# A hybrid decoder step on one core: half of the weight rests on GpSimd up to the MLP, the first weight blocks in halves, the convolution as a side job

## The chip, the cores and the metric

The kernel runs on one core of a Trainium2 chip. The metric is the device time of one execution in microseconds (us); less is better. Before the change three runs took 1318.51, 1319.54 and 1319.89 us, median 1319.54.

## The reference

One layer of a decoder for 256 prompt tokens and 8 x 8 sample tokens, 320 tokens in all, in float32, at a width of 2048:

```
z = rmsnorm(x, g_mix) @ w_in                      # 2048 x 3584: b, c, h, q, k, v, qx
u = c * h;  y_conv = b * short_conv(u, conv_w)    # three taps; the samples start from a cache
y_swa = sink_attention(rmsnorm(q), rmsnorm(k), v, rel_bias, sinks)   # window 128, 8 heads
mk, mv = rmsnorm(mem) @ w_mem_k (normed), @ w_mem_v                  # 256 memory tokens
y_x = softmax(rmsnorm(qx) mk) mv                  # 4 heads; the samples read a cache
x = x + concat(y_conv, y_swa, y_x) @ w_out        # 2048 x 2048
x = x + relu(rmsnorm(x, g_mlp) @ w_up)^2 @ w_down # 2048 x 8192, 8192 x 2048
```

Returned are x and the new cache rows (convolution, keys, values).

## The kernel before

**The matrix products.** Activations lie transposed, 16 blocks of 128 features by 320 tokens. Each float32 operand is split into a high part that the matmul's fp32r type holds exactly and the rest: `S0h`, `S0l` and `S1h`, `S1l` for activations, `wh`, `wl` for weights. A product is three matmuls, high x high, low x high and high x low, the last of which reads `wl`.

**Weight pieces.** The weights come in 360 pieces of 256 rows x 512 columns (512 KB). `load_piece` starts the transfer of a piece into one of four `raw` tiles on SP's queue. `split_piece` has ScalarE write `wh` (`act.activation ... Copy`) and notes a function `rest`, in which VectorE writes `wl = raw - wh` and which then starts the load of the piece four further on into the `raw` tile that this frees. Four `wh`/`wl` pairs exist, so the split of piece i waits for the last matmul on piece i - 4.

**Units.** A group is 512 output columns, four PSUM tiles `mm` (m = 0 to 3); it takes 8 pieces (`w_out` in two parts of 4). `add_group` cuts it into units of 12 matmuls: at a group's start and end one m with two pieces, between them two m with one piece. The very first group starts with units of two m and one piece. `run_unit` issues a unit, then calls `split_piece` and `boundary`, which lets the due evacuations and rests be issued and steps the side jobs. The groups in order: qx, then k and v, the memory keys and values (matmuls of 512 columns), q (two groups), c, h, b, `w_out`, and four times `w_up` and `w_down`. `split_piece` starts with pieces 0 and 1; the first of them is split in two halves.

**Side jobs.** Everything else on TensorE (norms, attention, transposes, in PSUM tiles `ax`) is a Python generator that `Side.step` moves on by a step between units. A job waits in its program position until `Pace`, a model with a clock for each engine and a cost for each operation, says that its tiles are ready (`after`). The model decides only where an instruction stands in the order; on the chip each engine executes its own instructions in that order and waits on semaphores. `bias_job` builds the relative bias: transfers on GpSimd's queue, then a matmul `ax<-w,z` on the tile `hot` that holds `in_c_hot`. Its `dve.memset` of `bt` stands in VectorE's order after the rest of piece 7, and the transfers on GpSimd's queue wait for it.

**The convolution.** `c_evac` and `h_evac` run when the groups c and h end. `h_evac` for each m forms h, multiplies it into `u` and applies the three taps at once, on VectorE. `b_evac` multiplies by b.

**Where things are recorded.** All operations are issued through `Paced`, so that nearly all rows of the profile have one line, L166. Tiles tell them apart.

Of the kernel before, what the change touches and what calls it, by code (L numbers as in the profile page):

```python
# [9 lines left out]
F32 = mybir.dt.float32  # L10
# [23 lines left out]
NW2 = 12  # L34
LAG = 6.0
WARM = 9
C_B, C_C, C_H, C_Q, C_K, C_V, C_X = 0, 512, 1024, 1536, 2560, 2816, 3072
# [55 lines left out]
class Pace:  # L93
# [12 lines left out]
    def cost(self, eng, op, out, ins):  # L106
        n = max(a.free_size() for a in [out] + ins)
        if eng == "pe":
            n = out.free_size()
            if ins[0].dtype == F32R:  # L110
                return 0.0033 + n / 2400.0
            quarter = 0.25 if out.partition_size() == 32 else 1.0
            return 0.0009 * n if op == "transpose" else max(0.11, n / 600.0) * quarter
        if eng == "act":
            return 0.1 + n * 0.00083
        if eng == "dve":
            return 0.08 + n * 0.00104
        return 0.1 + n * 0.0025
# [15 lines left out]

    def load(self, out):
        start = max(self.clock["dma"], self.clock["pe"])
        self.clock["dma"] = start + out.free_size() * 4 * out.partition_size() / 330e3
        self.wrote[out.name] = (self.clock["dma"] + (2.0 if out.name.startswith("raw") else LAG), "dma")

# [7 lines left out]
class Paced:  # L147
# [3 lines left out]
    def __getattr__(self, op):  # L151
        f = getattr(self.engine, op)
        if not callable(f) or op == "preload_act_table_set":
            return f

        def issue(*args, **kw):
            aps = [a for a in list(kw.values()) + list(args) if isinstance(a, bass.AP)]
            out = kw["out"] if "out" in kw else args[0]
            if op == "dma_start":
                if out.name not in self.pace.dram:  # L160
                    self.pace.load(out)
            else:
                if "accum_out" in kw:
                    self.pace.wrote[kw["accum_out"].name] = (self.pace.clock[self.name] + 0.5, self.name)
                self.pace.issue(self.name, op, out, [a for a in aps if a is not out])
            return f(*args, **kw)  # L166

        return issue
# [79 lines left out]
def trunk_step(ctx: ExitStack, tc: tile.TileContext, I, O):  # L248
# [26 lines left out]

    def bank():
        return ax.need([P, 512])

# [18 lines left out]
    ident = const.tile([P, P], F32, name="ident")  # L297
    act.dma_start(out=ident, in_=I["c_ident"])
    col, off = {}, 0
# [96 lines left out]
    def load_piece():  # L396
        i = count["load"]
        if i >= len(pieces):
            return
        count["load"] += 1  # L400
        w, k0, c0 = pieces[i]
        t = raw_p.tile([P, 2, 512], F32, name="raw", tag="raw")
        for c in [slice(0, 2)] if i else [slice(0, 1), slice(1, 2)]:
            sp.dma_start(out=t[:, c, :], in_=w[c0 // 512, k0 // 2][:, c, :])
        wt[i] = t

    def split_piece():
# [8 lines left out]
        wt[i] = (h, l)  # L416
        if not i:
            for c in range(2):
                side.until([f"x0{c}"])
                act.activation(out=h[:, c, :], in_=r[:, c, :], func=AF.Copy)  # L420
                dve.tensor_tensor(out=l[:, c, :], in0=r[:, c, :], in1=h[:, c, :].bitcast(F32), op=ALU.subtract)
            load_piece()
# [9 lines left out]
    def add_group(w, c0, korder, a, evac, kind="std", needs=None, pre=None, k0=0):  # L432
# [36 lines left out]
    def run_unit(un):  # L469
# [9 lines left out]
        ah, al = un["act"]()  # L479
        if un["kind"] == "std":  # L480
            for m in un["ms"]:
# [38 lines left out]

    def load_x(b, cuts=((0, 4),)):
        t = lx.must([P, 4, T])
        for lo, hi in cuts:
            sp.dma_start(out=t[:, lo:hi, :], in_=I["xT"][:, 4 * b + lo:4 * b + hi, :])
        xblk[b] = t

# [9 lines left out]
    def x_job():  # L536
        for i in range(8):
            for k in (2 * i, 2 * i + 1):
                split_act(S0h[:, k, :], S0l[:, k, :], xblk[k // 4][:, k % 4, :], gcol("g_mix", k))
                if not i:  # L540
                    side.flags.add(f"x0{k}")
                    yield 1
            side.flags.add(f"x{i}")
            yield 1
# [294 lines left out]
    def cross_sample(f):  # L839
# [92 lines left out]
    def swa_prompt(g, hp):  # L932
# [7 lines left out]
        for blk in range(2):  # L940
# [20 lines left out]
            yield 1  # L961
            pt = yield from half()
            act.activation(out=pt[:, 0:2 * nk], in_=bk[:, 0:2 * nk], func=AF.Copy)
            ax.put(bk)
            w2.put(s)
            yield from after(pt, vnat)
# [146 lines left out]
    def conv_pre_job():  # L1113
        st["u"] = yield from lx.need([P, 4, UC])
        cc = yield from half()
        pool.memset(st["u"][:, :, 0:2], 0.0)
        sp.dma_start(out=cc[:, 0:64], in_=I["cconv"].rearrange("p m r -> p (m r)"))
        yield from after(cc)
# [3 lines left out]
        w2.put(cc)  # L1122

    def h_evac(m, ps):
# [28 lines left out]
    def b_evac(m, ps):  # L1153
        side.until(["cp"])
        y = st["y"][m]
# [148 lines left out]
    side.add("cp", cross_prompt_all(), needs=xq + ["mk", "mix"], cost=2, heavy=1)  # L1304
    side.add("convpre", conv_pre_job(), needs=["rb", "mix"], cost=1)
    side.add("cs1", cross_sample(1), needs=xq + ["cs0"], cost=6, heavy=2)
    for g in range(2):
        qn = [f"q{g * 4 + h}" for h in range(4)]
        for i in range(2):
            side.add(f"swp{g}{i}", swa_prompt(g, i), needs=qn + [f"k{g}", f"v{g}", "bias", "cp"], cost=3, heavy=1)  # L1310
    for g in range(2):
        qn = [f"q{g * 4 + h}" for h in range(4)]
        for i in range(2):
            side.add(f"sws{g}{i}", swa_sample(i, g), needs=qn + [f"k{g}", f"v{g}", "biass", "cp"], cost=2, heavy=1)

    split_piece()
    side.until(["x1"])
    split_piece()
    flush(subs)
    for un in units:  # L1320
# [46 lines left out]
```

## Time and profile before

| what | value |
|---|---|
| profiled execution | 1319.31 us, span 1316.8 us |
| runs shown | 1318.51, 1319.54, 1319.89 us |
| TensorE busy | 1309.4 us, 8954 matmul records |
| VectorE busy | 675.2 us |
| ScalarE busy | 540.5 us |
| GpSimd busy | 17.7 us, 36 instructions |
| granted TensorE clock | 1.0 over the span |

2.5 us of the profiled execution lie outside its span. A matmul's record reaches from its start to its modelled end and overlaps the next one, so TensorE's pace is read from the distance of the starts, and a wait of TensorE from a distance that is larger than the pace. "[0.78 <-DMA w<-in_c_hot]" behind a row of the timeline says how long the engine was idle before it and what ended that. In such rows `w`, `z`, `lx`, `ax`, `mm` are families of buffers.

### The profile page before, as it was taken

Reading aid. Unit: us, or ns where it says so; the run is one execution under the profiler, and the core shown is the slowest. Engines: PE = TensorE matmul, PEld = TensorE weight load, DVE = VectorE, ACT = ScalarE, POOL = GpSimd, SP = SyncE. Lnnn points to the kernel's source line nnn. Section 1 sums busy time; section 2 is a strip of 40 time slices with the busy share of each in tenths; the row PEclk is TensorE's granted clock in tenths of the full one; section 3 lists DMA queues with packets and bytes.
Section 4 is the critical chain, followed back from the end, with each engine's and each line's share of the span. In section 5 each row is a group of like instructions: output and inputs, shape, how many; then the busy total and the mean of one; then the engine's idle time right before and its main releaser. Section 6 shows DMA issues by size and latency. Waiting matters only on the chain.

```text
span 1316.8 us, 21550 instructions
## 1 busy us (share of the span) xinstructions
PE 1309.4 (99%) x8954; PEld 1286.9 (98%) x8954; DVE 675.2 (51%) x1022; ACT 540.5 (41%) x801; POOL 17.7 (1%) x36
## 2 busy tenths in 40 slices
PE   9999999999999999999999999999999999999998
PEld 8988999999999999999999999999999999999998
DVE  6876666776576444444344444344443344444342
ACT  7784554343355344332244432234442324433321
POOL 1011000000000000000000000000000000000000
PEclk9999999999999999999999999999999999999999
DMA  8667545366344444444444444444444444444552
GB/s 310 240 200 267 189 165 200 109 220 250 128 145 161 145 152 136 160 147 158 146 155 133 152 159 154 147 157 129 160 154 152 153 151 128 161 154 152 176 167 72
DMA packets 65025, 217.03 MB, mean 165 GB/s; under 512 B 8374, under 2 KB 10142, under 8 KB 64897
## 3 DMA queue, kind: packets, MB, share of 16 engines
q1 hardware_dynamic: 62896, 210.38, 47.8%
q0 software_dynamic: 1744, 5.19, 1.1%
q8 instruction: 70, 1.15, 0.4%
q14 instruction: 27, 0.21, 0.0%
q10 hardware_dynamic: 288, 0.10, 0.0%
HBM read 211.53 MB, written 7.65 MB: 166 GB/s over the span
## 4 chain that ended last, share of the span: by engine, by line
PE 98%; DMA 1%; DVE 0%; SPq 0%; ACT 0%; issue 0%; POOL 0%; DVEq 0%
PE mm L166 95%; PE ax L166 3%; DMA raw<-in_w_in 0%; DMA w<-in_c_hot 0%; DVE wl L166 0%; SPq L166 0%; ACT wh L166 0%; POOL z L166 0%; DVE lx L166 0%; DVE S0l L166 0%; DVEq L166 0%; DVE z L166 0%
## 5 line engine op out<-in xcount | busy, mean ns | idle before, releaser
L166 DVE TENSOR_TENSOR wl<-raw,wh 128x1024 fp32r<-128x1024 f32 (+1 forms) x361 | 435.9, 1220 | 479.8 <-ACT wh L166 473.2
L166 ACT ACTIVATE wh<-raw 128x1024 fp32r<-128x1024 f32 (+1 forms) x361 | 374.1, 1052 | 629.5 <-PE mm L166 591.0
L166 PE MATMUL mm<-S0h,wh 128*128 128x320 f32 x1472 | 458.1, 311 | 0.4 <-ACT wh L166 0.4
L166 PE MATMUL mm<-S0h,wl 128*128 128x320 f32 x1472 | 455.3, 309 | 1.6 <-DVE wl L166 1.6
L166 PE MATMUL mm<-S0l,wh 128*128 128x320 f32 x1472 | 454.8, 309 | 0.0
L166 PE MATMUL mm<-S1h,wh 128*128 128x320 f32 x1280 | 397.3, 310 | 0.0
L166 PE MATMUL mm<-S1h,wl 128*128 128x320 f32 x1280 | 395.5, 309 | 0.0
L166 PE MATMUL mm<-S1l,wh 128*128 128x320 f32 x1280 | 395.5, 309 | 0.0
L166 PEld LDWEIGHTS mm<-S0h,wh 128*128 128x128 f32 x1472 | 276.4, 188 | 3.8 <-issue 2.7
L166 PEld LDWEIGHTS mm<-S0h,wl 128*128 128x128 f32 x1472 | 276.3, 188 | 2.6 <-DVE wl L166 2.6
L166 PEld LDWEIGHTS mm<-S0l,wh 128*128 128x128 f32 x1472 | 276.5, 188 | 0.1
L166 PEld LDWEIGHTS mm<-S1h,wh 128*128 128x128 f32 x1280 | 240.3, 188 | 0.7 <-issue 0.6
L166 PEld LDWEIGHTS mm<-S1l,wh 128*128 128x128 f32 x1280 | 240.3, 188 | 0.1
L166 PEld LDWEIGHTS mm<-S1h,wl 128*128 128x128 f32 x1280 | 240.2, 188 | 0.0
L166 DVE TENSOR_TENSOR lx<-mm,lx 128x320 f32<-128x320 f32 x96 | 46.9, 489 | 78.7 <-PE mm L166 78.6
L166 ACT ACTIVATE z<-z 128x320 f32<-128x320 f32 (+1 forms) x118 | 54.9, 469 | 65.3 <-DVE z L166 64.2
L166 DVE TENSOR_TENSOR S1l<-z,S1h 128x320 fp32r<-128x320 f32 x68 | 33.4, 491 | 51.8 <-ACT S1h L166 51.8
L166 ACT ACTIVATE S1h<-z 128x320 fp32r<-128x320 f32 x68 | 32.1, 471 | 8.1 <-DVE z L166 6.1
L166 DVE SCALAR_TENSOR_TENSOR z<-mm,r2b 128x320 f32<-128x320 f32 x64 | 31.0, 484 | 0.0
L166 PE MATMUL mm<-wh,S1h 128*128 128x512 f32 x64 | 25.6, 400 | 0.0
L166 PE MATMUL mm<-wh,S1l 128*128 128x512 f32 x64 | 25.1, 392 | 0.0
L166 PE MATMUL mm<-wl,S1h 128*128 128x512 f32 x64 | 25.0, 391 | 0.0
(160 smaller groups left out, 431.2 us busy)
## 6 DMA issues: line engine op xcount, KB each, us to landing
raw<-in_w_up SPq DMA_DIRECT2D x128, 512.0 KB, 3.3
raw<-in_w_down SPq DMA_DIRECT2D x128, 512.0 KB, 3.3
raw<-in_w_in SPq DMA_DIRECT2D x55, 512.0 KB, 4.3
raw<-in_w_out SPq DMA_DIRECT2D x32, 512.0 KB, 3.5
raw<-in_w_mem_k SPq DMA_DIRECT2D x8, 512.0 KB, 4.5
raw<-in_w_mem_v SPq DMA_DIRECT2D x8, 512.0 KB, 3.4
w<-in_cmk SPq DMA_DIRECT2D x16, 256.0 KB, 5.3
w<-in_cmv SPq DMA_DIRECT2D x16, 256.0 KB, 5.2
```

Source lines behind the costliest of these rows:

```text
L166: return f(*args, **kw)
```

## The change

1. **Rests on GpSimd.** For the even pieces 8 to 102 (48 of them) `rest` issues `wl = raw - wh` on GpSimd in place of VectorE.
2. **The start.** Pieces 0 and 1 are both split in halves, with the activation blocks 0 to 3 split between the halves; the transfers are issued block by block in the order in which they are used, the first of x on ScalarE's queue. The first four units take one half of a piece for all four m, as four high x high, four low x high and four high x low matmuls. Ten in place of nine warming matmuls on `ones` stand ahead. `ident` is loaded on GpSimd's queue.
3. **Model.** The costs in `Pace` are changed, a transfer that is issued on GpSimd's queue counts as ready after 10 us in place of 6, others after 5; that moves side jobs in the order.
4. **Convolution.** The three taps leave `h_evac` for a side job, `conv_job`. The cache rows of the convolution are loaded with the bias.
5. **Smaller moves.** The x blocks that `w_out` adds to are loaded one group at a time. Two memsets go from GpSimd to VectorE. The last of the 16 output blocks is added and stored in two halves, on two queues.

```diff
-LAG = 6.0
-WARM = 9
+LAG = 5.0
+WARM = 10
+POOLED = 8, 104
...
-        if not i:
+        if i < 2:
+
             for c in range(2):
-                side.until([f"x0{c}"])
+                k = 2 * i + c
+                x = xblk[0][:, k, :]
+                if k:
+                    split_act(S0h[:, k, :], S0l[:, k, :], x, gcol("g_mix", k))
+                else:
+                    dve.tensor_scalar(out=S0h[:, k, :], in0=x, scalar1=gcol("g_mix", k), scalar2=None, op0=ALU.mult)
+                    dve.scalar_tensor_tensor(out=S0l[:, k, :], in0=x, scalar=gcol("g_mix", k),
+                                             in1=S0h[:, k, :].bitcast(F32), op0=ALU.mult, op1=ALU.subtract)
                 act.activation(out=h[:, c, :], in_=r[:, c, :], func=AF.Copy)
                 dve.tensor_tensor(out=l[:, c, :], in0=r[:, c, :], in1=h[:, c, :].bitcast(F32), op=ALU.subtract)
...
+        eng = pool if not i % 2 and POOLED[0] <= i < POOLED[1] else dve
+
         def rest():
-            dve.tensor_tensor(out=l, in0=r, in1=h.bitcast(F32), op=ALU.subtract)
+            eng.tensor_tensor(out=l, in0=r, in1=h.bitcast(F32), op=ALU.subtract)
             load_piece()
...
-                ends[0] = [([2 * q, 2 * q + 1], [i]) for i in range(2) for q in range(2)]
+                ends[0] = [(list(range(4)), [i]) for i in range(2) for _ in range(2)]
...
+            for n, (w, x) in enumerate(((h, ah), (h, al), (l, ah))):
+                for m in un["ms"]:
+                    pe.matmul(out=grp[m][:, 0:T], lhsT=w[:, j, m * P:(m + 1) * P], rhs=x[:, k, :],
+                              start=u == 0 and n == 0, stop=False)
...
         dve.memset(bt[0:33, 0:8], 1.0)
+        pool.dma_start(out=ident, in_=I["c_ident"])
         pool.dma_start(out=bt[0:32, 0:8], in_=I["rel_bias_table"])
         pool.dma_start(out=hot[0:33, 0:384], in_=I["c_hot"])
         pool.dma_start(out=skb, in_=I["sinks"].to_broadcast([P, NH]))
         pool.dma_start(out=sel, in_=I["c_sel"])
+        pool.dma_start(out=cc, in_=I["cconv"].rearrange("p m r -> p (m r)"))
         pool.dma_start(out=gkx, in_=I["g_k_x"].to_broadcast([P, P]))
...
-        dve.tensor_scalar(out=z, in0=u[:, m, 0:336], scalar1=gcol("conv_w", m), scalar2=None, op0=ALU.mult)
-        for i in (1, 2):
-            dve.scalar_tensor_tensor(out=z, in0=u[:, m, i:i + 336], scalar=gcol("conv_w", 4 * i + m), in1=z,
-                                     op0=ALU.mult, op1=ALU.add)
-        st["y"][m] = z
+        zs.put(z)
         if m == 3:
-            side.add("convout", conv_out_job())
+            side.add("convy", conv_job())
...
+            if last and g == 3 and m == 3:
+                for queue, c in ((act, slice(0, T // 2)), (sp, slice(T // 2, T))):
+                    dve.tensor_tensor(out=a[:, c], in0=ps[:, c], in1=a[:, c], op=ALU.add)
+                    queue.dma_start(out=O["yT"][:, KT - 1, c], in_=a[:, c])
+                return
...
-    load_x(0, ((0, 2),))
+    load_x(0, 0, 1, act)
     load_piece()
-    sp.dma_start(out=xblk[0][:, 2:4, :], in_=I["xT"][:, 2:4, :])
     load_piece()
-    load_x(1, ((0, 2), (2, 4)))
+    for k in range(4):
+        if k:
+            load_x(0, k, k + 1, sp)
+        load_part(k // 2, slice(k % 2, k % 2 + 1))
+    load_x(1, 0, 2, sp)
     load_piece()
...
```

How the change moves instructions, at the places on which the prediction rests. On GpSimd, before, from the transfers of the bias job (`z` is `bt`, `w_4` is `hot`) to the store of the biases:

```order
L166 DMA z_346<-in_rel_bias_table 32x8
L166 DMA w_4_347<-in_c_hot 33x384
L166 DMA skb<-in_sinks 128x8
L166 DMA sel<-in_c_sel 128x4
L166 DMA gkx<-in_g_k_x 128x128
L166 MEMSET w_5_435 128x512
L166 MEMSET w_6_436 128x512
L166 DMA rv_d<-w_11_486 8x384
```

And in the changed kernel:

```order
L169 DMA z_352<-in_rel_bias_table 32x8
L169 DMA w_4_353<-in_c_hot 33x384
L169 DMA skb<-in_sinks 128x8
L169 DMA sel<-in_c_sel 128x4
L169 DMA cc<-in_cconv 128x64
L169 DMA gkx<-in_g_k_x 128x128
L169 ISA
L169 TENSOR_TENSOR wl<-raw,wh 128x1024
L169 MEMSET w_5_445 128x512
L169 MEMSET w_6_446 128x512
L169 TENSOR_TENSOR wl<-raw,wh 128x1024
L169 DMA rv_d<-w_12_517 8x384
```

One transfer more, the first two rests (pieces 8 and 10), and ahead of the first of them an instruction of a kind of its own, ISA, which this place of the program before does not have. In the built program that row is a reload of GpSimd's code library, number 0.

On TensorE around the matmul of the bias, before: it stands behind 168 matmuls on weights, 24 ahead of the end of the first group:

```order
L166 MATMUL mm<-S0h,wh 128x320
L166 MATMUL mm<-S0l,wh 128x320
L166 MATMUL mm<-S0h,wl 128x320
L166 MATMUL ax_460<-w_4_347,z_346 8x384
L166 MATMUL mm<-S0h,wh 128x320
```

And in the changed kernel, where it stands behind 180:

```order
L169 MATMUL mm<-S0h,wh 128x320
L169 MATMUL mm<-S0l,wh 128x320
L169 MATMUL mm<-S0h,wl 128x320
L169 MATMUL ax_489<-w_4_353,z_352 8x384
L169 MATMUL mm<-S0h,wh 128x320
```

The twelve matmuls of one unit have moved ahead of it, and the rest of piece 8 is read 14 matmuls behind it in place of 26.

On VectorE in the group h, before, the last convolution of `h_evac` and the rests of pieces 66, 67 and 68:

```order
L166 TENSOR_TENSOR z_2944<-mm,rb 128x320
L166 TENSOR_TENSOR lx_1375<-z_2944,lx_1375 128x256
L166 TENSOR_TENSOR lx_1375<-z_2944,lx_1375 128x8x8
L166 TENSOR_SCALAR z_2944<-lx_1375,cols 128x336
L166 SCALAR_TENSOR_TENSOR z_2944<-lx_1375,cols,z_2944 128x336 x2
L166 TENSOR_TENSOR wl<-raw,wh 128x1024
```

And in the changed kernel:

```order
L169 TENSOR_TENSOR z_3029<-mm,rb 128x320
L169 TENSOR_TENSOR lx_1381<-z_3029,lx_1381 128x256
L169 TENSOR_TENSOR lx_1381<-z_3029,lx_1381 128x8x8
L169 TENSOR_SCALAR z_3036<-lx_1381,cols 128x336
L169 SCALAR_TENSOR_TENSOR z_3036<-lx_1381,cols,z_3036 128x336 x2
L169 TENSOR_TENSOR S1l<-ax_2957,S1h 128x4x32
L169 TENSOR_TENSOR S1l<-ax_2959,S1h 128x4x32
L169 TENSOR_TENSOR wl<-raw,wh 128x1024
```

The `wl` in the first of these is piece 66, in the second piece 67; piece 66 is now GpSimd's. Of the four convolutions one stands ahead of it in place of four.

More of the change, by code (lines that the diff above doesn't have):

```diff
@@ L133, in issue, with load @@
                 self.read[k] = (end, eng)
-    def load(self, out):
+    def load(self, out, queue):
         start = max(self.clock["dma"], self.clock["pe"])
-        self.clock["dma"] = start + out.free_size() * 4 * out.partition_size() / 330e3
-        self.wrote[out.name] = (self.clock["dma"] + (2.0 if out.name.startswith("raw") else LAG), "dma")
+        self.clock["dma"] = start + out.free_size() * 4 * out.partition_size() / 410e3
+        self.wrote[out.name] = (self.clock["dma"] + (2.0 if out.name.startswith("raw") else 2 * LAG if queue == "pool" else LAG), "dma")
     def ready(self, tiles):
@@ L160, in issue @@
                 if out.name not in self.pace.dram:
-                    self.pace.load(out)
+                    self.pace.load(out, self.name)
             else:
                 if "accum_out" in kw:
-                    self.pace.wrote[kw["accum_out"].name] = (self.pace.clock[self.name] + 0.5, self.name)
+                    self.pace.wrote[kw["accum_out"].name] = (self.pace.clock[self.name] + 0.9, self.name)
                 self.pace.issue(self.name, op, out, [a for a in aps if a is not out])
+                if "accum_out" in kw:
+                    self.pace.clock[self.name] += 0.19
             return f(*args, **kw)
@@ L274, in after, with bank @@
             yield 1
-    def bank():
-        return ax.need([P, 512])
+    def bank(every=1):
+        while side.now % every:
+            yield 1
+        t = ax.get([P, 512])
+        while t is None:
+            yield every
+            t = ax.get([P, 512])
+        return t
     def zt(cols=336):
@@ L400, in load_piece, with load_part @@
         count["load"] += 1
+        wt[i] = raw_p.tile([P, 2, 512], F32, name="raw", tag="raw")
+        if i > 1:
+            load_part(i, slice(0, 2))
+    def load_part(i, c):
         w, k0, c0 = pieces[i]
[L402 to L405, printed above, removed]
+        sp.dma_start(out=wt[i][:, c, :], in_=w[c0 // 512, k0 // 2][:, c, :])
     def split_piece():
@@ L519, in trunk_step, with load_x @@
     xblk, mblk = {}, {}
[L521 to L525, printed above, removed]
+    def load_x(b, lo, hi, queue):
+        if b not in xblk:
+            xblk[b] = lx.must([P, 4, T])
+        queue.dma_start(out=xblk[b][:, lo:hi, :], in_=I["xT"][:, 4 * b + lo:4 * b + hi, :])
     def load_m(i):
@@ L536, in x_job @@
     def x_job():
-        for i in range(8):
+        for i in range(2, 8):
             for k in (2 * i, 2 * i + 1):
                 split_act(S0h[:, k, :], S0l[:, k, :], xblk[k // 4][:, k % 4, :], gcol("g_mix", k))
-                if not i:
-                    side.flags.add(f"x0{k}")
-                    yield 1
             side.flags.add(f"x{i}")
@@ L1114, in conv_pre_job @@
         st["u"] = yield from lx.need([P, 4, UC])
[L1115 to L1118, printed above, removed]
+        dve.memset(st["u"][:, :, 0:2], 0.0)
         for m in range(4):
@@ L1132, in h_evac, with conv_job @@
         dve.tensor_tensor(out=us, in0=per_batch(z[:, TP:T]), in1=us, op=ALU.mult)
-        dve.tensor_scalar(out=z, in0=u[:, m, 0:336], scalar1=gcol("conv_w", m), scalar2=None, op0=ALU.mult)
-        for i in (1, 2):
-            dve.scalar_tensor_tensor(out=z, in0=u[:, m, i:i + 336], scalar=gcol("conv_w", 4 * i + m), in1=z,
-                                     op0=ALU.mult, op1=ALU.add)
-        st["y"][m] = z
-        if m == 3:
-            side.add("convout", conv_out_job())
+        zs.put(z)
+        if m == 3:
+            side.add("convy", conv_job())
+    def conv_job():
+        u = st["u"]
+        for m in range(4):
+            z = yield from zt()
+            dve.tensor_scalar(out=z, in0=u[:, m, 0:336], scalar1=gcol("conv_w", m), scalar2=None, op0=ALU.mult)
+            for i in (1, 2):
+                dve.scalar_tensor_tensor(out=z, in0=u[:, m, i:i + 336], scalar=gcol("conv_w", 4 * i + m), in1=z,
+                                         op0=ALU.mult, op1=ALU.add)
+            st["y"][m] = z
+            yield 2
+        side.add("convout", conv_out_job())
     def conv_out_job():
@@ L1153, in b_evac @@
     def b_evac(m, ps):
-        side.until(["cp"])
+        side.until(["cp", "convy"])
         y = st["y"][m]
@@ L1304, in trunk_step @@
     side.add("cp", cross_prompt_all(), needs=xq + ["mk", "mix"], cost=2, heavy=1)
-    side.add("convpre", conv_pre_job(), needs=["rb", "mix"], cost=1)
+    side.add("convpre", conv_pre_job(), needs=["rb", "mix"])
     side.add("cs1", cross_sample(1), needs=xq + ["cs0"], cost=6, heavy=2)
@@ L1309, in trunk_step @@
         for i in range(2):
-            side.add(f"swp{g}{i}", swa_prompt(g, i), needs=qn + [f"k{g}", f"v{g}", "bias", "cp"], cost=3, heavy=1)
+            side.add(f"swp{g}{i}", swa_prompt(g, i), needs=qn + [f"k{g}", f"v{g}", "bias", "cp"], cost=2, heavy=1)
     for g in range(2):
@@ L1313, in trunk_step @@
         for i in range(2):
-            side.add(f"sws{g}{i}", swa_sample(i, g), needs=qn + [f"k{g}", f"v{g}", "biass", "cp"], cost=2, heavy=1)
+            side.add(f"sws{g}{i}", swa_sample(i, g), needs=qn + [f"k{g}", f"v{g}", "biass"], cost=2, heavy=1)
     split_piece()
-    side.until(["x1"])
     split_piece()
-    flush(subs)
     for un in units:
```

33 lines of the change are left out of this document (21 added, 12 removed).

## The prediction

> **What bounds the kernel now.** I read the page's busy times and chain first, then the end of the chain of waits, then the waits of TensorE alone.
>
> ```profile
> span 1316.8 us, 21550 instructions
> PE 1309.4 (99%) x8954; PEld 1286.9 (98%) x8954; DVE 675.2 (51%) x1022; ACT 540.5 (41%) x801; POOL 17.7 (1%) x36
> PE 98%; DMA 1%; DVE 0%; SPq 0%; ACT 0%; issue 0%; POOL 0%; DVEq 0%
> 419.24 894.09 PE mm L166 x6096
> PE mm L166 <- DVE wl L166: 1.6, 3, 1.1
> PE ax L1292 <- DVE ones L166: 1.1, 1, 1.1
> PE ax L166 <- DMA w<-in_c_hot: 0.8, 1, 0.8
> PE mm L166 <- ACT wh L166: 0.4, 1, 0.4
> ```
>
> TensorE is the bound from start to end. Its pace is 894.09 / 6096 = 0.1467 us for a matmul of 320 columns, with no wait in the last 894 us. The change keeps every matmul, so it can win only what TensorE waits: the four rows add up to 3.9 us, and a slow start comes on top. Taking VectorE from 51% to less wins nothing by itself. A rest that comes later than TensorE wants it, on the other hand, costs its full lateness, once, since TensorE never catches up.
>
> TensorE's rows at the start, around the bias and at piece 8:
>
> ```profile
> 1.06 4.21 PE L1292 MATMUL ax<-ones 128*128 128x128 f32 x18 [1.06 <-DVE ones L166]
> 5.67 0.57 PE L166 MATMUL mm<-S0h,wh 128*128 128x320 f32 x1 [0.40 <-ACT wh L166]
> 6.65 0.41 PE L166 MATMUL mm<-S0h,wh 128*128 128x320 f32 x1
> 6.90 0.38 PE L166 MATMUL mm<-S0l,wh 128*128 128x320 f32 x1
> 7.46 0.41 PE L166 MATMUL mm<-S0h,wl 128*128 128x320 f32 x1 [0.19 <-DVE wl L166]
> 11.21 0.41 PE L166 MATMUL mm<-S0h,wl 128*128 128x320 f32 x1 [0.39 <-DVE wl L166]
> 33.07 0.80 PE L166 MATMUL ax<-w,z 33*8 33x384 f32 x2 [0.78 <-DMA w<-in_c_hot]
> 33.81 0.41 PE L166 MATMUL mm<-S0h,wh 128*128 128x320 f32 x1
> 37.72 0.31 PE L166 MATMUL mm<-S0h,wl 128*128 128x320 f32 x1
> ```
>
> The row at 11.21 is the 27th matmul on weights; at the pace the first would have started at 11.21 - 26 x 0.1467 = 7.4, not 5.67. The row at 37.72 is the first that reads the rest of piece 8.
>
> **Term 1, the start up to the bias.** The new start order puts four matmuls (0.6 us) ahead of each late operand, which covers the waits at 7.46 and 11.21; with x block 0 and ten warming matmuls (4.21 / 9 = 0.47 each, so until some 0.4 later than before) TensorE still starts at about 5.5. How much of this is kept is set by the bias matmul, which waits for `in_c_hot`. GpSimd's rows, and VectorE's memset that lets them go:
>
> ```profile
> 25.64 1.22 DVE L166 TENSOR_TENSOR wl<-raw,wh 128x1024 fp32r<-128x1024 f32 x1
> 26.80 0.07 DVE L166 MEMSET z<- 33x8 f32 x1
> 27.19 0.68 POOL L166 DMA_DIRECT2D z<-in_rel_bias_table  x1 [26.74 <-DVE z L166]
> 27.85 0.57 POOL L166 DMA_DIRECT2D w<-in_c_hot  x1
> 29.50 0.54 POOL L166 DMA_DIRECT2D gkx<-in_g_k_x  x1
> w<-in_c_hot POOLq DMA_DIRECT2D x1, 49.5 KB, 5.1
> ```
>
> The memset stands behind the rest of piece 7 in both kernels. Up to there ScalarE and VectorE follow the transfers of x and of the first eight pieces, which the change reorders and hardly lessens, so I leave the memset at 26.8 and the landing at 27.85 + 5.1 = 33.0. TensorE reaches the bias earlier (5.9 + 180 x 0.1467 = 32.3, with about 0.4 us lost to the low clock at the start) and still waits for it until 33.0; but 180 matmuls are done by then in place of 168. Gain 12 x 0.1467 = **-1.8**. Bounds: 0, if the memset comes as much later, and -2.7, if it comes earlier.
>
> **Term 2, the rest of piece 8.** The order shows GpSimd's queue behind the bias transfers: one transfer more (0.55), then the ISA row, then this rest. The queue reaches ISA at 29.50 + 0.54 + 0.55 = 30.6. TensorE reads this rest 14 matmuls behind the bias: 33.07 + 0.74 + 14 x 0.1467 = 35.9. So ISA and the rest have 5.3 us together. The trace has neither; the nearest rows:
>
> ```profile
> L1354 POOLq INC_SWDGE_SEM x1: 27/27/27, 0.1 to 0.1; - x1
> 1.18 1.28 ACT L296 ACT_TABLE_LOAD   x1 [1.18 <-PEq L1354]
> z<-in_rel_bias_table POOLq DMA_DIRECT2D x1, 1.0 KB, 5.6
> out_old_k<-in_cache_swa_k POOLq DMA_DIRECT2D x1, 960.0 KB, 8.8
> L166 POOL MEMSET w<- 128x512 f32 x6 | 3.2, 567 | 60.4 <-PE ax L166 60.4
> ```
>
> A reload of code is at least 0.03 us (GpSimd's other instruction that moves no data) and at most issue + longest read of this queue + a table load: 0.6 + 8.8 + 1.28 = 10.7. It resembles a small read on this queue and a table load, so I take 0.6 + 5.6 + 1.28 = 7.5, an estimate. The rest itself: at least VectorE's 1.22; at most three passes at the memset's speed, 3 x 2 x 0.567 = 3.4; I take two passes, 2.3. It ends at 30.6 + 7.5 + 2.3 = 40.4, so TensorE waits 4.5 us, and is at this matmul at 40.4 in place of 37.7. Terms 1 and 2 together: **+2.7** (bounds -1.8 without a wait, and 30.6 + 10.7 + 3.4 - 37.7 = +7.0).
>
> [...]
>
> Behind the rest stands a load:
>
> ```profile
> raw<-in_w_in SPq DMA_DIRECT2D x55, 512.0 KB, 4.3
> L166 ACT ACTIVATE wh<-raw 128x1024 fp32r<-128x1024 f32 (+1 forms) x361 | 374.1, 1052 | 629.5 <-PE mm L166 591.0
> ```
>
> `raw` 12 waits on SP's queue (issued at 40.4 in place of about 29.5), and behind that piece 13 and a memory block that ScalarE wants. TensorE reads piece 12 only 94 matmuls later, at 54.2; load (4.3), split (1.05) and rest (2.3) end at 48.1. That is hidden.
>
> **Term 3, the convolution.** VectorE and TensorE at the end of the group h:
>
> ```profile
> 256.84 0.48 DVE L166 TENSOR_TENSOR z<-mm,rb 128x320 f32<-128x320 f32 x1
> 258.38 1.18 DVE L166 SCALAR_TENSOR_TENSOR z<-lx,cols,z 128x336 f32<-128x336 f32 x2
> 259.48 1.22 DVE L166 TENSOR_TENSOR wl<-raw,wh 128x1024 fp32r<-128x1024 f32 x1
> 259.39 0.31 PE L166 MATMUL mm<-S0l,wh 128*128 128x320 f32 x1
> 260.75 0.42 PE L166 MATMUL mm<-S0h,wl 128*128 128x320 f32 x1 [1.05 <-DVE wl L166]
> ```
>
> The rest of piece 66 is queued behind four convolutions. It goes to GpSimd, which has nothing ahead of it, and three of the four move behind the next rest. TensorE's gap of 1.36 becomes 0.15: **-1.2** (bounds 0 and -1.2).
>
> **What I cost at nothing.** The two halves at the end:
>
> ```profile
> 1313.35 0.49 DVE L166 TENSOR_TENSOR lx<-mm,lx 128x320 f32<-128x320 f32 x1 [1.27 <-PE mm L166]
> out_yT<-lx SPq DMA_DIRECT2D x1, 160.0 KB, 1.8
> ```
>
> The second half is added no earlier than 0.49 behind the matmul, and stores land 1.8 us later whatever part of that is size: between -0.4 and +0.2, taken 0. The 48 rests that leave VectorE (58.6 us) and the moved side jobs are hidden by TensorE's matmuls; a side job's matmul that comes before its data costs like the bias's 0.8. The waits of GpSimd's later transfers (stores of keys, values, cache rows) delay the rests queued behind them by a few us, and splits run up to four pieces, 4 x 24 x 0.1467 = 14 us, ahead.
>
> **Sum.** 1319.31 + 2.7 - 1.2 = 1320.8 against the profiled execution, which lies 0.2 under the median of the runs; the difference of 0.2 is within their spread, and I leave 1320.8.
>
> **Rivals.**
>
> *The reload is nearly free* (it was resident, or runs in 2 us). For it: nothing but the ISA row says that it costs. Then no wait at piece 8: 1319.3 - 1.8 - 1.2 = 1316.3. Against it: code has to come from somewhere. Chance 0.20.
>
> *The reload is long, and the clock falls in the wait* (the slower side). Place: the same matmul. From 1.06 to 7.46 TensorE ran with matmuls 0.25 apart (6.65 to 6.90), afterwards at 0.147: after standing idle it needs about 6.4 us of work to get its full pace, which costs up to 6.4 x (1 - 0.147 / 0.25) = 2.6. With 10.7 for the reload the rest ends at 43.6, +5.9 with term 1: 1319.3 + 5.9 - 1.2 + 2.6 = 1326.6. It decides from a wait above the 1.2 that the trace shows without a fall. Against it: reload and clock would both have to be at their worst. Either alone gives 1323 to 1324. Chance of one or both 0.18.
>
> [...]
>
> *VectorE is held up by GpSimd's rests.* Where the rests come nearest to TensorE's need, VectorE was nearly full (a row of busy times by stretch: length, PE, PEld, DVE, ACT, POOL):
>
> ```profile
> 33.00:66.00 33.00, 32.93 (x221) 32.31 (x222) 27.31 (x48) 23.48 (x44) 1.65 (x2) 1.00 0.68 239
> ```
>
> In 33 us 4.7 rests move. If VectorE stood still during each of them, it would need 27.31 - 4.7 x 1.22 + 4.7 x 2.3 = 32.4 of the 33 us, and the rests that stay on it would come late; 2 us in sum is an estimate from this fill: 1322.8. Against it: the wait at piece 8 gives VectorE time to get ahead. Chance 0.08. [...]
>
> *A side job's place*, moved by the model's new costs, makes a new wait of 1 to 3 us: 0.04.
>
> **How the numbers follow.** The forecast, a wait of 2.5 to 6 us at piece 8 (a reload of 5.5 to 9), has 0.50 and by itself 1318.8 to 1322.3. A measurement here tells 0.2% from no change, 2.6 us: faster is below 1316.9, slower above 1322.2. Faster takes nearly all of the free reload (0.17) and a little of the forecast: 0.21. Slower takes the long reload, the lock and the forecast's upper end: 0.29. Same 0.50. The range 1316.2 to 1325.2 takes in the free reload and leaves out the worst of the long one.
>
> **What would show it.** Right: on TensorE a gap of 3 to 6 us that ends with GpSimd's `wl` near 40, GpSimd idle or loading from 30.6 to 38, 180 matmuls ahead of a bias matmul near 33.0, no gap at the rest of piece 66. Wrong: a gap below 1 us there (then the time is near 1316), `in_c_hot` landing at another time, matmuls 0.25 apart behind the gap, more than three further waits of TensorE for `wl` between 40 and 400, or VectorE's `wl` rows far longer than 1.22 while GpSimd forms one.

## The result: 1335.8 us, 1.2% slower

Four runs of the changed kernel took 1333.89 to 1336.17 us, median 1335.78; four of the kernel before, on the same chip, 1318.51 to 1319.89, median 1319.69. The ratio is 1.0122, 95% interval 1.0109 to 1.0134: 16 us slower, where the prediction had 1320.8 and a range up to 1325.2. The profiled execution took 1336.17 us, its span is 1334.4.

The page of the changed kernel: busy times, and GpSimd's busy share in tenths over 40 slices of the span:

```profile
span 1334.4 us, 21556 instructions
PE 1316.0 (99%) x8956; PEld 1289.6 (97%) x8956; DVE 684.8 (51%) x982; ACT 540.4 (41%) x801; POOL 132.1 (10%) x81
POOL 2342422232332000000000000000000000000000
```

VectorE executes 40 instructions fewer than before and yet is busy for 9.6 us more, although 48 rests of 1.22 us each have left it. That is the first sign. TensorE's rows at the start, at the bias and at the first matmul that reads the rest of piece 8, and GpSimd's rows between them (timeline of the changed kernel; start, length, engine, instruction, and in brackets the idle time before it):

```profile
5.55 0.72 PE L169 MATMUL mm<-S0h,wh 128*128 128x320 f32 x2
...
29.72 0.56 POOL L169 DMA_DIRECT2D gkx<-in_g_k_x  x1
30.36 2.46 POOL L169 TENSOR_TENSOR wl<-raw,wh 128x1024 fp32r<-128x1024 f32 x1
33.01 0.81 PE L169 MATMUL ax<-w,z 33*8 33x384 f32 x2
35.90 0.31 PE L169 MATMUL mm<-S0h,wl 128*128 128x320 f32 x1
```

The first rest on GpSimd begins 0.08 us after the last issue of a transfer ends, and is done at 32.82, 3.1 us before TensorE reads it. In that gap, where the ISA row stands in the order, GpSimd's queue has two short rows (in ns, and their time in us):

```profile
L169 POOLq MODIFY_POOL_CONFIG  x2: 59/59/59, 30.3 to 30.3; - x2
```

That is all that is seen of a reload. Before the bias matmul stand 180 matmuls in place of 168 at the same time (33.01 and 33.07). Up to here the change wins what was hoped for. The waits of TensorE after that (engine, tile and what it waited for; total, times, longest):

```profile
PE ax L169 <- DVE z L169: 3.3, 4, 1.5
PE ax L169 <- ACT z L169: 3.2, 1, 3.2
PE ax L169 <- DMA w<-in_cmk: 3.1, 1, 3.1
PE ax L169 <- DVE S1l L169: 1.2, 1, 1.2
```

No rest, neither GpSimd's nor VectorE's, is in the list, and no line on the rest of piece 66. All of the long waits are at `ax`, matmuls of side jobs. Against the kernel before, the changed one is 1.9 us ahead at the 181st matmul on weights, the first behind the bias, 5.1 us behind at the 385th, 16.3 at the 540th (some 120 us into the kernel), 17.7 at the 1908th, and 17.7 at the last one: the loss arises ahead of the MLP, most of it in the first tenth.

Why the side jobs are late shows in VectorE's groups by shape between 30 and 350 us. Kernel before:

```profile
L166 DVE SCALAR_TENSOR_TENSOR S1l<-w,cols,S1h 128x256 fp32r<-128x256 f32 x16 | 7.4, 479 | 0.6 <-ACT S1h L166 0.6
L166 DVE TENSOR_TENSOR z<-z,z 128x320 fp32r<-128x320 f32 x14 | 6.7, 485 | 0.0
L166 DVE TENSOR_TENSOR sm<-sm,nskb 128x2 f32<-128x2 f32 x8 | 1.3, 160 | 0.3
L166 DVE TENSOR_TENSOR z<-mm,rb 128x320 f32<-128x320 f32 x20 | 9.8, 488 | 7.4 <-PE mm L166 7.3
```

Changed kernel:

```profile
L169 DVE SCALAR_TENSOR_TENSOR S1l<-w,cols,S1h 128x256 fp32r<-128x256 f32 x16 | 17.2, 1079 | 5.2 <-ACT S1h L169 5.2
L169 DVE TENSOR_TENSOR z<-z,z 128x320 fp32r<-128x320 f32 x14 | 12.5, 906 | 7.9 <-ACT z L169 7.8
L169 DVE TENSOR_TENSOR sm<-sm,nskb 128x2 f32<-128x2 f32 x8 | 7.4, 924 | 0.3
L169 DVE TENSOR_TENSOR z<-mm,rb 128x320 f32<-128x320 f32 x20 | 9.7, 487 | 6.0 <-PE mm L169 6.0
L169 POOL TENSOR_TENSOR wl<-raw,wh 128x1024 fp32r<-128x1024 f32 x48 | 115.8, 2413 | 246.2 <-ACT wh L169 238.6
```

Instructions of the same shape and operation take twice as long, one on two columns (160 ns) nearly six times. The fourth row is as before (488 and 487 ns): one of its inputs, `mm`, lies in PSUM. So are the other groups of this stretch with an input in PSUM, such as `z<-ax,z` of 128x320 (485 and 482) and `lx<-mm,lx` (488 and 490). The groups that are stretched take both inputs from SBUF, a few others aside (below). Two places in the timeline of the changed kernel show how:

```profile
61.35 2.37 POOL L169 TENSOR_TENSOR wl<-raw,wh 128x1024 fp32r<-128x1024 f32 x1 [5.53 <-ACT wh L169]
61.70 2.30 DVE L169 SCALAR_TENSOR_TENSOR S1l<-w,cols,S1h 128x256 fp32r<-128x256 f32 x1 [0.46 <-ACT S1h L169]
64.43 0.63 ACT L169 ACTIVATE w<-w 128x512 f32<-128x512 f32 x1 [0.98 <-DVE S1l L169]
64.97 0.45 ACT L169 ACTIVATE z<-z 128x320 fp32r<-128x320 f32 x1
65.47 0.94 PE L169 MATMUL ax<-z,mean_h 128*128 128x320 f32 x2 [3.22 <-ACT z L169]
...
281.36 2.39 POOL L169 TENSOR_TENSOR wl<-raw,wh 128x1024 fp32r<-128x1024 f32 x1 [6.30 <-ACT wh L169]
281.65 2.12 DVE L169 TENSOR_TENSOR sm<-sm,nskb 128x2 f32<-128x2 f32 x1
```

VectorE's `sm`, 0.16 us of work, begins during GpSimd's rest and ends with it: 281.65 + 2.12 = 283.77, and 281.36 + 2.39 = 283.75. At 61.70 it is `S1l`, 0.48 us of work, that ends 0.3 us behind GpSimd's rest (64.00 and 63.72). The second half of `S1l` follows, ScalarE's `w` waits for that (64.43), ScalarE's `z` stands behind `w` in its order, and TensorE, which had come to the matmul on `z` 3.22 us earlier, waits for all of it. This is a hold of VectorE by GpSimd, and the last link before TensorE is a side job's chain, not a weight piece.

The other wait of 3 us, for `in_cmk`, has a different last link (GpSimd's row from the timeline, the others from the chain that ended last):

```profile
108.02 2.41 POOL L169 TENSOR_TENSOR wl<-raw,wh 128x1024 fp32r<-128x1024 f32 x1 [8.21 <-ACT wh L169]
108.92 2.60 DVE wl L169
111.92 1.36 SPq L169
113.33 4.90 DMA w<-in_cmk
```

VectorE's own rest begins during GpSimd's and takes 2.60 us in place of 1.22. The loads of two weight pieces wait on SP's queue for these two rests, and the transfers of `in_cmk` stand behind the loads. So a held rest can also make a transfer late that has nothing to do with it.

How long VectorE stood still in all follows from the busy times: with all rests on VectorE the same kernel has 676.0 us (the first experiment below); less 48 x 1.222 that is 617.3, and 684.8 were measured. That leaves **67.5 us**, 1.4 us for each of GpSimd's rests, which cost VectorE more than the 1.22 us that forming one itself does.

Last, the granted clock of TensorE by stretch of time (stretch; length; PE, PEld, DVE, ACT, POOL busy; clock; DMA share; GB/s), changed kernel:

```profile
60.00:65.00 5.00, 2.26 (x16) 1.99 (x14) 4.54 (x6) 3.81 (x7) 2.37 (x1) 1.00 0.63 240
65.00:70.00 5.00, 4.42 (x20) 4.19 (x21) 4.03 (x9) 3.71 (x10) 0.00 (x0) 0.74 0.70 251
115.00:120.00 5.00, 2.35 (x14) 0.66 (x16) 1.67 (x5) 0.00 (x0) 0.00 (x0) 0.86 1.01 362
120.00:125.00 5.00, 5.00 (x22) 3.60 (x17) 0.58 (x2) 1.95 (x3) 0.86 (x1) 0.80 0.74 285
```

Behind each of the two waits of 3 us TensorE also runs at a lower clock for a few us; taken finer, the clock is 0.50 from 67.50 to 70.80 and from 118.60 to 121.90. The long distances between the starts of matmuls (over 0.6 us) add up to 16.7 us in the changed kernel and to 4.0 before; the other 5 of the 17.7 us are shorter distances, part of them at this clock (0.27 us in place of 0.147 between the starts from 67.7 to 70.6).

### The profile page after: what moved, and what is told of

It reads as the page before. It is cut to its first block, busy times and chain, and to the rows that moved or that the text cites. A ratio compares the mean times of both kernels' runs of the same rounds, so it can differ in the third digit from the quotient of the medians.

```text
span 1334.4 us, 21556 instructions
## 1 busy us (share of the span) xinstructions
PE 1316.0 (99%) x8956; PEld 1289.6 (97%) x8956; DVE 684.8 (51%) x982; ACT 540.4 (41%) x801; POOL 132.1 (10%) x81
## 4 chain that ended last, share of the span: by engine, by line
PE 89%; DVE 3%; DMA 3%; issue 2%; ACT 1%; POOL 1%; SPq 0%; DVEq 0%; POOLq 0%; ACTq 0%
PE mm L169 86%; PE ax L169 3%; POOL wl L169 1%; ACT wh L169 1%; DMA raw<-in_w_in 1%; DVE z L169 1%; DMA w<-in_cmk 1%; DMA raw<-in_w_mem_k 1%; DVE sm L169 1%; DVE wl L169 1%; DVE lx L169 0%; DMA w<-in_cmv 0%; SPq L169 0%; DMA rv_d<-w 0%; DVE S1l L169 0%
## 5 line engine op out<-in xcount | busy, mean ns | idle before, releaser
L169 DVE TENSOR_TENSOR wl<-raw,wh 128x1024 fp32r<-128x1024 f32 (+1 forms) x314 | 386.1, 1242 | 446.8 <-ACT wh L169 445.8
L169 POOL TENSOR_TENSOR wl<-raw,wh 128x1024 fp32r<-128x1024 f32 x48 | 115.8, 2413 | 246.2 <-ACT wh L169 238.6
L169 DVE TENSOR_TENSOR lx<-mm,lx 128x320 f32<-128x320 f32 (+1 forms) x97 | 47.0, 486 | 97.8 <-PE mm L169 97.8
L169 DVE SCALAR_TENSOR_TENSOR S0l<-lx,cols,S0h 128x320 fp32r<-128x320 f32 x32 | 21.7, 696 | 7.0 <-ACT S0h L169 6.9
```

## The experiments

Two theories at first. **L**: VectorE's instructions with two inputs from SBUF stand still while GpSimd forms a rest. **M**: the new costs in the planner place side jobs' matmuls ahead of their data, and GpSimd's rests do no harm. All ratios are against runs of the kernel before on the same chip, whose median lay between 1319.2 and 1319.3 us.

**1. The change with its rests on VectorE.**

```diff
-POOLED = 8, 104
+POOLED = 0, 0
```

> The changed kernel with all rests on VectorE; start, model, convolution job and small moves stay. Theory L (a rest on GpSimd holds VectorE's instructions that read two SBUF operands, so side jobs come late and TensorE waits for them): nearly the whole loss goes, and the start (-1.7) and the rest of piece 66 (-1.2) stay won: 1316 to 1318, no tiny VectorE instruction above 1 us. Theory M (the model's new costs put the side jobs' matmuls ahead of their data): the waits of TensorE for z and for in_cmk stay, 1328 to 1336.

Measured: 1320.16 us, ratio 1.0009 (1.0001 to 1.0018). VectorE's rows are back at 480, 485 and 161 ns. 15.6 of the 16 us go with the rests on GpSimd. The other parts of the change together win nothing, where I had expected 1316 to 1318; this is followed up in runs 13 and 14.

**2. The rests on GpSimd alone, in the kernel before.**

```diff
+POOLED = 8, 104
...
+        eng = pool if not i % 2 and POOLED[0] <= i < POOLED[1] else dve
+
         def rest():
-            dve.tensor_tensor(out=l, in0=r, in1=h.bitcast(F32), op=ALU.subtract)
+            eng.tensor_tensor(out=l, in0=r, in1=h.bitcast(F32), op=ALU.subtract)
```

> The kernel before with nothing but the 48 rests moved to GpSimd. L: slower than before by 8 to 20 us, with VectorE rows of 2 us and more for small instructions that read two SBUF operands. M: within 2 us of before, 1318 to 1321.

Measured: 1342.09 us, 1.0174 (1.0160 to 1.0188), 22.8 us lost, more than the 8 to 20 expected, with the planner's old costs and all else in the program as before. TensorE's largest waits are of the same kind, and one is now at `mm`, for an evacuation:

```profile
PE ax L167 <- ACT z L167: 6.7, 2, 5.5
PE mm L167 <- DVE lx L167: 3.2, 2, 2.9
PE ax L167 <- DVE z L167: 2.8, 2, 2.5
```

**3. The change with the planner's old costs.**

```diff
-LAG = 5.0
+LAG = 6.0
...
-                return 0.0135 + n / 2400.0
+                return 0.0033 + n / 2400.0
...
-            return 0.16 + n * 0.00105
+            return 0.08 + n * 0.00104
```

(and so for ScalarE's costs, the accumulator and the transfers.)

> The changed kernel with the model's old numbers (6 us for every transfer, the old costs), rests still on GpSimd. L: still slow, 1328 to 1340, with the waits at other side jobs. M: the loss goes, 1316 to 1320.

Measured: 1337.15 us, 1.0134 (1.0119 to 1.0150), 1.4 us from the changed kernel. The new costs aren't the cause.

**4. The same, with the rests on VectorE.**

```diff
-POOLED = 8, 104
+POOLED = 0, 0
```

> Old model numbers and all rests on VectorE; of the change the start, the convolution job and the small moves are left. L: like the run with the rests on VectorE and the new model, 1316 to 1319. M: clearly faster than that run, 1316 to 1318 against 1328 or more. Both: the start shows its -1.7 by the matmul of the bias.

Measured: 1318.14 us, 0.9992 (0.9983 to 1.0001). Theory L stands, M falls as the main cause. This is the fastest kernel of the study, though its interval just reaches no change.

One thing these four runs do not separate. The planner counts a rest on the engine that forms it, so whoever moves the rests also moves side jobs: from the 385th matmul record on, TensorE's order in run 1 is not the changed kernel's. How much of the 15.6 us is the hold and how much the other order is therefore open here. Runs 9 to 12 all have run 1's order on TensorE, matmul by matmul, and run 7 has the changed kernel's.

**5 and 6. What on GpSimd holds VectorE?** Rests on VectorE, and GpSimd with spare work beside each even piece: 4 writes, or 4 one-input reads, gated by a copy of one column out of the piece's rounded half. (`POOLED = 0, 0` and `IDLE = 8, 104` here and in runs 9 to 12, where one tile of constants is also used twice to make room.)

```diff
             eng.tensor_tensor(out=l, in0=r, in1=h.bitcast(F32), op=ALU.subtract)
+            if not i % 2 and IDLE[0] <= i < IDLE[1]:
+                nc.gpsimd.tensor_copy(out=s1[:, 0:1], in_=h[:, 0, 0:1].bitcast(F32))
+                for _ in range(4):
+                    nc.gpsimd.memset(s1, 0.0)
```

(run 6: `nc.gpsimd.tensor_copy(out=s1, in_=h[:, c, :].bitcast(F32))` for c = 0, 1, 0, 1.)

> All rests on VectorE as in the run with the rests taken off GpSimd (1320.2 us), and GpSimd instead writes 4 times 128x512 of zeros into a spare tile beside each of the 48 even pieces, about 2.3 us by the 567 ns row of its 128x512 memset in the profile before; nothing else is changed or left out. If only GpSimd's reading of SBUF holds VectorE up, nothing is lost: 1318 to 1323 us. If any access of GpSimd to SBUF does, VectorE's two-input instructions stretch as in the changed kernel: 1330 to 1345 us.

> The same, with 4 copies of 128x512 out of the piece's rounded half in the place of the 4 memsets: one input, read from SBUF, result thrown away. If reading with one input is enough to hold VectorE up, the loss comes back though VectorE has all its rests: 1327 to 1345 us, with VectorE's sm<-sm,nskb and S1l<-w,cols,S1h stretched. If GpSimd must read two inputs for it, 1318 to 1323 us and those rows as in the kernel before.

Measured: 1335.78 us, 1.0124 (1.0109 to 1.0140), with writes, and 1351.61 us, 1.0247 (1.0233 to 1.0261), with reads. By the times, writes would hold VectorE too, but the rows deny it: with writes `S1l`, `z<-z,z` and `sm` take 480, 485 and 161 ns, as without. ScalarE's waits in the run with writes tell what went wrong:

```profile
ACT wh L170 <- POOL s L455: 7.8, 4, 2.6
```

The gate reads the rounded half, so ScalarE's next rounding into that buffer had to wait for GpSimd, and what reads that half came late. The times of these two runs say nothing on the holds; the next four leave that tie out.

**7. Each of GpSimd's rests in two instructions.**

```diff
-            eng.tensor_tensor(out=l, in0=r, in1=h.bitcast(F32), op=ALU.subtract)
+            for c in ((0, 1) if eng is pool else (slice(0, 2),)):
+                eng.tensor_tensor(out=l[:, c, :], in0=r[:, c, :], in1=h[:, c, :].bitcast(F32), op=ALU.subtract)
```

> The changed kernel with each of GpSimd's rests in two instructions of 128x512. If VectorE waits for the GpSimd instruction in progress and is let in between two of them, a hold is at most about 1.2 us instead of 2.4 and some half of the loss goes: 1326 to 1331 us. [...]

Measured: 1337.34 us, 1.0137 (1.0123 to 1.0150), above the 1326 to 1331 expected: nothing is won. VectorE's single instructions are stretched less (`S1l` 799 in place of 1079 ns, `sm` 280 in place of 924), but there are 96 instructions on GpSimd in place of 48, and VectorE's busy time is 673.7 us, still 56 us above 617.3. GpSimd's own time grows: a half takes 1407 ns on the mean, so 2.81 us for a piece in place of 2.41:

```profile
L169 POOL TENSOR_TENSOR wl<-raw,wh 128x512 fp32r<-128x512 f32 x96 | 132.8, 1407 | 231.7 <-ACT wh L169 204.6 <-PE ax L169 18.2 <-PE mm L169 8.7
```

**8. GpSimd's rests from piece 24 on.**

```diff
-POOLED = 8, 104
+POOLED = 24, 104
```

> The changed kernel with GpSimd forming rests only from piece 24 on, 40 of the 48. If every rest on GpSimd costs the same, 40/48 of the loss of 16 us stays: 1331 to 1334 us. If only those rests cost that fall into the first 340 us, where side jobs' chains on VectorE must be done in time, the loss is nearly gone: 1318 to 1323 us, with TensorE's gaps of over 1.2 us before piece 24 gone.

Measured: 1326.37 us, 1.0052 (1.0039 to 1.0064), between the two expectations. The first 8 of the 48 rests cost 9.4 us, 1.2 us each, the other 40 together 6.2, or 0.16 each, with the order that the planner makes of each choice. VectorE still stands still for 43.8 us (670.9 less 676.0 - 40 x 1.222), two thirds of what it was, so the time lost does not follow the sum of the holds. I read it so that a hold costs what it makes a side job late, and that early on, where VectorE was the fullest, this is most of it; no run here shows that step by itself.

**9 to 12. The hold by itself.** Rests on VectorE; ScalarE writes a column of its own for each even piece from 8 to 102, GpSimd copies it and then does spare work on a tile that nobody else uses.

```diff
         act.activation(out=h, in_=r, func=AF.Copy)
+        if not i % 2 and IDLE[0] <= i < IDLE[1]:
+            nc.scalar.activation(out=go[:, i // 2 - 4:i // 2 - 3], in_=ones_h[:, 0:1], func=AF.Copy)
+            nc.gpsimd.tensor_copy(out=s1[:, 0:1], in_=go[:, i // 2 - 4:i // 2 - 3])
+            for _ in range(7):
+                nc.gpsimd.memset(s1, 0.0)
```

(run 9 without the last two lines; run 11 with 5 times `tensor_copy(out=s1, in_=s1)`, run 12 with 4 times `tensor_tensor(out=s1, in0=s1, in1=s1, op=ALU.subtract)` in their place.)

> The control of the next three runs: all rests on VectorE (1320.2 us), and behind each even piece's rounded half from 8 to 102 ScalarE writes one column into a spare tile, a column of its own each time, which GpSimd copies (one element per partition). Nothing waits for GpSimd here, in difference to the two runs with spare writes and spare reads before, where ScalarE's next rounded half could wait for GpSimd. Both theories: 1318 to 1324 us.

> The control plus 7 memsets of 128x256 on GpSimd behind each of the 48 copies, about 2.3 us that write SBUF and read nothing. If writes don't hold VectorE, within 2 us of the control and VectorE's two-input rows between 30 and 350 us as before (S1l<-w,cols,S1h 0.48 us, z<-z,z 0.485 us). If the 16 us that the run with spare writes lost came from GpSimd's writing itself, 1330 us and more here too.

> The control plus 5 copies of 128x256 on GpSimd (in place in the spare tile) behind each of the 48, about 2 us that read one input from SBUF. If reading one input holds VectorE, 3 to 12 us over the control, since each hold is short, with z<-z,z 128x320 between 0.6 and 0.8 us as with the spare reads before (0.72). If the loss there came only from ScalarE's waits for GpSimd, within 2 us of the control.

> The control plus 4 subtractions of 128x256 on GpSimd behind each of the 48 (both inputs the spare tile), about 2.5 us that read two inputs from SBUF, as a rest does. If reading is what holds VectorE and two inputs hold it longer, 8 to 20 us over the control, with VectorE's two-input rows stretched about as in the changed kernel with its rests in halves (S1l<-w,cols,S1h 0.80, z<-z,z 0.68 us). If it is the rest's own wait on the pieces that cost the time, within 2 us of the control.

| run | GpSimd's spare work | us | ratio | VectorE busy, us |
|---|---|---|---|---|
| 9 | none | 1319.85 | 1.0008 (0.9999 to 1.0018) | 676.5 |
| 10 | writes, 105.4 us | 1319.63 | 1.0003 (0.9994 to 1.0013) | 676.9 |
| 11 | reads of one input, 156.5 us | 1323.05 | 1.0031 (1.0019 to 1.0043) | 691.4 |
| 12 | reads of two inputs, 169.5 us | 1331.88 | 1.0103 (1.0086 to 1.0120) | 711.8 |

VectorE's and TensorE's instructions are the same in all four, in the same order. VectorE's group `z<-z,z` between 30 and 350 us, with writes:

```profile
L170 DVE TENSOR_TENSOR z<-z,z 128x320 fp32r<-128x320 f32 x14 | 6.5, 485 | 0.7 <-ACT z L170 0.7
```

With reads of one input:

```profile
L170 DVE TENSOR_TENSOR z<-z,z 128x320 fp32r<-128x320 f32 x14 | 8.0, 597 | 0.7 <-ACT z L170 0.7
```

With reads of two:

```profile
L170 DVE TENSOR_TENSOR z<-z,z 128x320 fp32r<-128x320 f32 x14 | 9.8, 722 | 0.7 <-ACT z L170 0.7
```

105 us of writes cost nothing; reading does, and by this the same kernel loses 3 and 12 us though GpSimd's work is of no use to anybody. That is the hold, alone, without any change in who waits for a weight or in the order: 12.0 us for 35.3 us of standing still (711.8 less 676.5). It shows the mechanism, not the whole sum: in the changed kernel VectorE stands still for nearly twice as long, in another order.

**13 and 14. Where does the start's gain go?** Run 13 is run 1 with the old costs of transfers in the planner; run 14 the kernel before with the new start, the new tail and the early load of the convolution's cache alone.

```diff
-LAG = 5.0
+LAG = 6.0
...
-        self.clock["dma"] = start + out.free_size() * 4 * out.partition_size() / 410e3
+        self.clock["dma"] = start + out.free_size() * 4 * out.partition_size() / 330e3
```

(Run 13, and GpSimd's queue as the others. Run 14 is run 4 with the taps back in `h_evac` and the attention's needs and the residual's loads as before.)

> The kernel with all rests on VectorE, with the old costs of a transfer in the planner (a lag of 6 us, 330 bytes a ns, GpSimd's queue as the others); the new costs of the engines stay. If the start's 1.9 us are given back where side jobs meet late transfers (TensorE waits 2.3 us at 110 us for in_cmk there), they are kept now: 1317 to 1318.5 us. If they are lost elsewhere, 1319 to 1321 us.

> The kernel before with the change's start (first blocks in halves, first two pieces by quarters, WARM 10, ident on GpSimd's queue), its tail and its early load of the convolution's cache alone: rests on VectorE, old costs, convolution in the evacuation, the attention's side jobs and the residual as before. If the moved side jobs give the start's gain back, 1317 to 1318 us (1319.3 less the 1.9 of the start). If any other order of the side jobs costs TensorE a few waits of about 1 us, 1318 to 1319.5 us, as the old costs with the moves (1318.1).

Measured: 1331.79 us, 1.0091 (1.0077 to 1.0104), and 1323.52 us, 1.0031 (1.0018 to 1.0043). Both miss. TensorE's waits in run 13, and its windows around the longest one:

```profile
PE ax L169 <- DVE w L169: 5.7, 1, 5.7
PE ax L169 <- DMA w<-in_c_hot: 3.1, 1, 3.1
```

```profile
355.00:360.00 5.00, 0.55 (x3) 0.14 (x1) 4.86 (x10) 2.37 (x10) 0.00 (x0) 0.92 0.11 34
360.00:365.00 5.00, 3.75 (x13) 3.01 (x14) 2.93 (x15) 2.38 (x7) 0.00 (x0) 0.50 0.18 71
365.00:370.00 5.00, 4.25 (x23) 3.63 (x22) 2.27 (x4) 2.70 (x5) 0.00 (x0) 0.90 0.00 0
```

The bias matmul now stands behind 156 matmuls on weights, and waits 3.1 us for a transfer that comes when it always did; and at 355 us the last attention jobs come together with no matmuls between them, so that TensorE waits 5.7 us for VectorE and goes on at a granted clock of 0.50 (360 to 365). From the 1908th to the 2160th matmul alone this order loses 14 us. In run 14 the kernel is still 1.9 us ahead at the 1000th matmul on weights, and 1.6 behind at the 1400th: in between lies the group h with its taps in the evacuation, for which TensorE waits four times. By the 1908th it is 4.6 behind.

```profile
PE mm L167 <- DVE z L167: 2.9, 4, 1.4
PE ax L167 <- DVE S1l L167: 1.5, 1, 1.5
```

So the start's gain isn't given back at one place by one part. It is real, and every new order of the side jobs has waits of its own, which here came to between nothing and 12 us. In run 1 they are 1.6 us for `in_cmk` and 0.8 for `z`. Which single move in run 1 costs its gain stays open.

**15. A planner that knows the holds.**

```diff
+        pair = len(ins) > 1 and op in ("tensor_tensor", "scalar_tensor_tensor") and \
+            not any(a.name[:2] in ("mm", "ax") for a in ins)
+        if eng == "dve" and pair:
+            for s, e in self.held:
+                if s <= start < e:
+                    start = e
...
+        if eng == "pool" and pair:
+            self.held = self.held[-3:] + [(start, end)]
```

> The changed kernel with a planner in which a VectorE instruction with two inputs outside PSUM that would begin during one of GpSimd's rests begins at its end; nothing else is changed. If the loss is one of order, TensorE's waits at side jobs' matmuls go and most of the 16 us come back: 1319 to 1324 us. If the holds themselves make the chains longer than the work that covers them, 1330 to 1337 us.

Measured: 1331.07 us, 1.0089 (1.0075 to 1.0103). The second expectation holds, just. 4.7 us come back, within what another order alone can do by runs 13 and 14. The holds remain: VectorE is busy for 678.3 us, 61 above 617.3. Its largest waits:

```profile
PE mm L178 <- DVE z L178: 3.0, 1, 3.0
PE ax L178 <- DMA w<-in_cmk: 2.8, 3, 1.7
PE ax L178 <- DMA w<-in_csk: 1.8, 1, 1.8
```

## Why the prediction was wrong

**What bounds the kernel** was right: TensorE from start to end, and what it waits is lost for good. The waits came at another place.

**Term 1** (-1.8) was right to 0.1: 180 matmuls ahead of a bias matmul at 33.01, 1.9 us ahead at the first matmul on weights behind it. Its 0.4 us for a low clock at the start, like the second rival's 6.4 us of slow work, was an estimate from matmuls 0.25 us apart; the granted clock reads 1.00 in all stretches from 0 to 12 us of the kernel before.

**Term 2** (+4.5) was wrong. The reload was taken at 7.5 us from a small read on that queue and a table load; it shows as two rows of 59 ns in a gap of 0.08. The rest itself was taken at 2.3 and took 2.41. TensorE doesn't wait there at all, as the first rival had it. The three durations from which the reload was put together were of other things. GpSimd's first subtraction in this program begins at 30.36, 0.08 us behind the instruction before it; whether its code lay ready by then the profile does not tell.

**Term 3** (-1.2) was right at its place: TensorE has no wait at the rest of piece 66 any more. Terms 1 and 3 together promised 3.0 us; with the rests on VectorE the whole change measures +0.9 on the medians. What failed here is that a gain at one place was carried to the end unchanged while the side jobs were reordered behind it.

**"What I cost at nothing"** is the step that decided: "the 48 rests that leave VectorE (58.6 us) and the moved side jobs are hidden by TensorE's matmuls". The 58.6 us didn't leave: VectorE stands still for 67.5 us, and the rests on GpSimd cost 15.6 us of the kernel's time (22.8 without the rest of the change), the order that the planner makes of them included. With the order held fixed, 35.3 us of standing still cost 12.0 us in run 12. So the step that failed is a term put at nothing because TensorE's matmuls would cover it; they do not cover a side job's chain that VectorE finishes late.

**The third rival**, VectorE held up by GpSimd's rests, named the right mechanism, with a chance of 0.08 and a price of 2 us. Its mistake is in the working: 4.7 rests in the 33 us were summed up against VectorE's free time, 32.4 of 33, as if only a full engine could make anybody late. But VectorE's instructions stand in chains with ScalarE and with SP's loads, at whose end a side job's matmul stands at a fixed place in TensorE's order. The `S1l` that was held for 2.3 us at 61.70 stood in the chain of TensorE's longest wait, 3.2 us, whatever the fill was. And the rival looked at one stretch of 33 us, where the 40 rests behind piece 24 still cost 6 us. The sign that I named, further waits of TensorE for `wl`, was at the wrong tile: none of its waits is for `wl`, and nearly all are at `ax`. The other sign, stretched rows of VectorE, was there, though least of all at the `wl` rows that I named (1249 ns on the mean over the whole kernel, 1328 between 30 and 350 us).

**The side jobs' place** (0.04), as the new costs move it, wasn't the cause, by runs 3 and 4; what moving the rests does to it stays open. It was priced too low as a risk: run 13 shows an order that costs 12 us.

## What to carry to other kernels

Moving two-input work to GpSimd did not free VectorE here, whose work has many two-input instructions on SBUF: 1.4 us of standing still for each 1.22 us taken away. Price such a move as if VectorE did the work all the same, and look for what waits on VectorE's chains, not at how full it is. The signs in this profile were one shape of instruction whose mean grew (`z<-z,z` from 485 to 906 ns) while its like with an input in PSUM stayed (`z<-mm,rb`, 488 and 487), and a busy time that did not fall when work was taken away (675.2 and 684.8 us). Where GpSimd only writes, as in run 10, no loss was measured (1319.63 us beside 1319.85 in run 9).

## What the runs showed of the hardware

- GpSimd's subtraction of 128x1024 takes 2.41 us beside VectorE's 1.22, and it costs VectorE 1.4 us of standing still on the average. Cutting it into two of 128x512 makes it 2 x 1.41 on the mean, and VectorE's loss 56 in place of 67.5 us (run 7).
- Not only instructions with two full inputs are stretched: VectorE's `z<-z,sm` of 128x192, a multiplication by a column with one full input, went from 320 to 808 ns in the changed kernel, and to 368 even with GpSimd's writes alone (run 10; 321 in run 9). Why writes stretch it no run here shows.
- The granted clock fell to 0.50 behind the waits of 3.2 and 3.1 us (67.50 to 70.80 and 118.60 to 121.90 in the changed kernel) and behind one of 5.7 (360 to 365 in run 13); behind a wait of 1.5 us, which ends at 87.61 in the changed kernel, it stayed at 1.00 (85 to 95). The mean over the span is 0.997 in run 8, where the longest wait of TensorE was 2.4 us, and 1.0 in run 14, where it was 1.5. How long a wait must be to lower the clock these runs do not settle.
